# Attention's matmuls inside a product instead of between two products, in a hybrid decoder block

## The chip, the cores and the metric

The kernel runs on one core of a Trainium2 chip. The time is the device time of one execution in microseconds (us), and the number compared is the median over several runs of the same program. A run that is profiled also leaves a trace, in which every instruction of the core's engines has a start and a duration: PE (TensorE matmuls), PEld (TensorE weight loads), DVE (VectorE), ACT (ScalarE), POOL (GpSimd) and SP (SyncE, which only issues DMAs here).

## What is computed

One layer of a decoder block on a sequence of 2048 positions with 1024 channels, in float32. Cut to what matters:

```python
h = rms_norm(x, norm_g)
u = h @ w_in                       # (2048, 1024) @ (1024, 8704)
v_c, b_c, c_c, z_c, q, k, v, z_a, gate_logits = split(u)
y_c = b_c * causal_depthwise_conv(c_c * v_c, conv_w) * silu(z_c)
y_a = y_c @ w_conv_out
q, k = rms_norm(q, per head), rms_norm(k, per head)     # 16 query heads, 4 key heads of 64
o = sliding_window_attention(q, k, v, sinks) * silu(z_a)  # window 128, blocks of 128
y_b = o @ w_attn_out
g_a, g_b = split(sigmoid(gate_logits + gate_b))
out = x + (g_a * y_a + g_b * y_b) @ w_out
```

In the attention each block of 128 queries meets its own block of keys and the one before it: scores, a mask, a softmax with one sink for each head, and the product of the probabilities with the values.

## The kernel before

**Precision.** A float32 operand is split into a high and a low part (fp32r), and a product is the sum of three matmuls: high with high, high with low, low with high. Every matmul comes with its own weight load of 128x128.

**Projections.** The sequence is worked in two tiles (t = 0 and 1) of 1024 positions. A projection of 256 output channels by 1024 positions is a unit. A unit is computed with seven products instead of eight, on sums of quarters of its operands. One product (`product`, line 454) is twelve matmuls of 128x512 into one PSUM bank: four chunks of the contraction by the three terms above. Between the products ACT and DVE copy, add and evacuate the banks (X, V and the single bank Y).

**The order of the work.** `run` (line 734) steps through the units. One step, a *tick*, issues one product on TensorE and then the tasks that stand in a table for this tick: every other task of the program was put there by `put(tick, task)`, and the table `PLACES` shifts some of them by a few ticks. All engines work in program order, so a task's place in the table is its place in the queue of each engine that it uses. Waits between engines are semaphores that follow from the tiles: an instruction that writes a tile waits for the last readers of what was in that buffer.

**Attention.** There are 64 blocks of attention work (2 tiles, 4 key heads, 8 blocks of 128 positions, all four query heads of the key head at once). Each is a chain of tasks, set from a tick n:

- n-5: `att_load`, DMAs on SP bring the queries and keys (tiles `q2`, `kq`, and `lows`, which has two fixed buffers).
- n: `att_scores` (line 1090). Six matmuls, the *scores*, are issued in a row: for each half h one of 128x384 (line 1099) and two of 128x192 (line 1103), into a PSUM tile `s` of two banks. The pool `ps_s` has a single buffer of it. Then DVE masks the tile, takes the row maxima (a reduction that reads `s`) and four small operations.
- n+1: `att_exp` (line 1125 and 1128). ACT computes the exponentials out of `s`, four instructions of 128x128, each followed by the read of its sum (ACTIVATION_READ_ACCUMULATOR). After the last of them the tile `s` is free.
- n+2 to n+10: DVE normalizes and transposes in 32x32 squares, POOL sends the result through DRAM (`fd`) and back (`x`), ACT and DVE split it, and POOL cuts it to the window with four selections (line 1175), the last of which completes `xl`.
- n+13: `att_values` (line 1186). Six matmuls of 128x256 in a row, the *values*, into a bank `po` of the pool `ps_m` with three buffers.
- n+14: `att_out` (line 1197): ACT copies two quarters of `po`; n+15: DVE adds the other two and SP stores.

A row of matmuls that a task issues stands on TensorE after the product of its tick and before the product of the next one. So in the program order of TensorE the scores stand as six in a row between two products, and so do the values.

Of the kernel before, what the change touches and what calls it, by code (L numbers as in the profile page):

```python
# [8 lines left out]
F32 = mybir.dt.float32  # L9
# [6 lines left out]
P = 128  # L16
# [5 lines left out]
NB = T // P  # L22
# [3 lines left out]
HD = 64  # L26
# [63 lines left out]
        (1, (1, 1), (1, 1), (0, 0)), (3, (1, 0), (1, 0), (1, 1)))  # L90
LD_SUM, SUM_STEP, Z_SUM = 3, 1, 1
N_ROOT, N_RB, N_STEP, W_AT = 36, 2, 10, 18
OP_FROM, OP_STEP, OP_LD = 3, 2, 5

V_, F_, B_, X_, L_, O_, S_ = 4, 2, 4, 9, 10, 13, 15
# [4 lines left out]
def block_kernel(  # L100
# [350 lines left out]

    B_AT = {(0, 0): 1, (1, 0): 2, (0, 1): 8, (1, 1): 3}

    def product(ps, u, n, ops, start):
        force(u, n)
        hi, lo = ready[u][n]
        for j in range(KP):
            b = ops[n][j]
            for i, (w, m) in enumerate(((hi, 0), (hi, 1), (lo, 0))):
                nc.tensor.matmul(  # L460
                    ps, lhsT=w[:, j, :], rhs=b[:, m, :],
                    start=start and j == 0 and i == 0, stop=j == KP - 1 and i == 2,
                    skip_group_check=not start)
        d = done.setdefault(u, set())
        d.add(n)
        live[0] -= sum(c for m, c in USES if n in m and m <= d)
# [267 lines left out]
    def run(gen):  # L734
        while True:
            tick[0] += 1
            if next(gen, gen) is gen:
                tick[0] -= 1
                return
            ahead_loads()  # L740
            hi, lo = (piece() if tick[0] >= W_FROM else None) or (None, None)
            if hi:
                hi()

            fs = at.pop(tick[0], [])
# [341 lines left out]
        nc.sync.dma_start(v4[LH].rearrange("p (i x) -> p i x", i=2), pairs)  # L1087
        return v2

    def att_scores(t, j, b, ld):  # L1090
        first = t * NB + b == 0
        nm = f"{t}_{j}_{b}"
        q2, kq, kz = ld
        rv = rqs[t, j][:, b // HB, b % HB]
        sp = ps_s.tile([P, 2, 2, 2 * P], F32, tag="s", name=f"s{nm}")
        for h in range(2):
            skip = (2 - h) * HD if first else 0
            keys = slice(h * HD + skip, (h + 3) * HD)
            nc.tensor.matmul(
                sp[:, h, :, skip : 3 * HD], lhsT=kq[:, 1, h * P : (h + 1) * P], rhs=kz[:, :, keys],  # L1100
                start=True, stop=False)
            for c in range(2):
                nc.tensor.matmul(  # L1103
                    sp[:, h, c, skip : 3 * HD], lhsT=q2[:, h, c, :], rhs=kq[:, 0, keys],
                    start=False, stop=c == 1)
# [14 lines left out]
        add(st[:, 2], sink_r[:, j].rearrange("p h c -> p (h c)"), st[:, 1])  # L1120
        return sg, st, rv
# [63 lines left out]

    def att_values(t, j, b, pcv, v2):
        xh, xl, y = pcv
        po = mbank(f"po{t}_{j}_{b}").rearrange("p g q -> p (g q)")
        for h in range(2):
            cs = slice(h * 2 * P, (h + 1) * 2 * P)  # L1190
            for n, (kind, xx) in enumerate(((2 + h, xh), (h, y), (2 + h, xl))):
                nc.tensor.matmul(  # L1192
                    po[:, cs], lhsT=v2[:, kind, :], rhs=xx[:, h],
                    start=n == 0, stop=n == 2)
        return po

    def att_out(t, j, b, po):
        pov = po.rearrange("p (h e s c q) -> p h e s c q", h=2, e=2, s=2, c=2)
        o = slot([P, 2, P], F32, f"o{t}_{j}_{b}")
        parts = []  # L1200
        for e in range(2):
            own, oth = HALVES[e], HALVES[1 - e]
            ov = o[own].rearrange("p c (h s q) -> p h s c q", h=2, s=2)
            nc.scalar.copy(ov, pov[oth, :, e])  # L1204
            parts.append((ov, pov[own, :, e]))
        return o, parts
# [526 lines left out]
    def attention(t, places):  # L1733
        for r, n in enumerate(places):
            j, b = divmod(r, NB)
            got = {}
            n += PLACES.get(f"a{t}.{r}", 0)

            def step(k, f, got=got):
                def g():  # L1740
                    got[k] = f(got)
                return g

            put(n - 5, step("l", lambda g, j=j, b=b: att_load(t, j, b)), f"a{t}.{r}.l")
# [219 lines left out]
```

## Time and profile before

| | |
|---|---|
| median of 3 runs | 1906.28 us (1903.66 to 1906.4) |
| profiled execution, its own time | 1902.79 us |
| its span, first to last instruction | 1901.1 us |
| PE busy | 1886.4 us of the span, 8646 matmuls |
| DVE, ACT, POOL busy | 1588.3, 1000.3, 646.1 us |
| granted TensorE clock | 1.000 |
| score matmuls / value matmuls | 384 / 384, in 64 rows of six each |

The page of the profile gives busy time for each engine, the waits give who waited for whom and how long, and the timeline gives single instructions: start, duration, engine, line of the code, operation, tile written and tiles read, shapes, and in brackets the idle time just before it with what ended it. Two things are to be kept in mind. Matmuls are pipelined and their recorded ends are modelled, so what a matmul costs is read from start to start, not from its duration. And the idle time of an engine that others do not wait for costs nothing.

### The profile page before, as it was taken

Reading aid. Unit: us, or ns where it says so; the run is one execution under the profiler, and the core shown is the slowest. Engines: PE = TensorE matmul, PEld = TensorE weight load, DVE = VectorE, ACT = ScalarE, POOL = GpSimd, SP = SyncE. Lnnn points to the kernel's source line nnn. Section 1 sums busy time; section 2 is a strip of 40 time slices with the busy share of each in tenths; the row PEclk is TensorE's granted clock in tenths of the full one; section 3 lists DMA queues with packets and bytes.
Section 4 is the critical chain, followed back from the end, with each engine's and each line's share of the span. In section 5 each row is a group of like instructions: output and inputs, shape, how many; then the busy total and the mean of one; then the engine's idle time right before and its main releaser. Section 6 shows DMA issues by size and latency. Waiting matters only on the chain.

```text
span 1901.1 us, 27689 instructions
## 1 busy us (share of the span) xinstructions
PE 1886.4 (99%) x8646; PEld 1567.7 (82%) x8646; DVE 1588.3 (84%) x2670; ACT 1000.3 (53%) x1989; POOL 646.1 (34%) x930
## 2 busy tenths in 40 slices
PE   9999999999999999999999999999999999999999
PEld 7888888888888888888878888888887888888887
DVE  7989989898889889877799888888888868878654
ACT  7565455457767345435465554556665435535221
POOL 2073335335565001123273444445565001223000
PEclk9999999999999999999999999999999999999999
DMA  8286555568888966778387554578887844879553
GB/s 307 65 240 190 157 158 171 172 196 281 252 251 253 314 238 210 253 185 263 101 236 215 164 166 146 162 222 261 285 250 228 280 151 152 274 167 290 187 173 108
DMA packets 228644, 398.05 MB, mean 209 GB/s; under 512 B 31312, under 2 KB 106064, under 8 KB 228496
## 3 DMA queue, kind: packets, MB, share of 16 engines
q1 hardware_dynamic: 191104, 295.27, 47.9%
q0 software_dynamic: 37248, 100.97, 19.5%
q8 instruction: 69, 1.13, 0.3%
q14 instruction: 79, 0.65, 0.1%
q10 hardware_dynamic: 144, 0.03, 0.0%
HBM read 264.80 MB, written 131.35 MB: 208 GB/s over the span
## 4 chain that ended last, share of the span: by engine, by line
PE 55%; issue 6%; DMA 3%; DVE 3%; POOL 2%; ACT 1%; SPq 0%; POOLq 0%; DVEq 0%; ACTq 0%
PE Y L460 19%; PE Vcv L460 2%; PE Xcv L460 2%; PE Vo L460 2%; PE Xo L460 2%; PE Vza L460 2%; PE Xza L460 2%; PE yb L1399 2%; PE Vya L460 1%; PE Vz L460 1%; PE Xz L460 1%; PE Vb L460 1%; PE Yya L460 1%; PE Xga L460 1%; PE Vga L460 1%
## 5 line engine op out<-in xcount | busy, mean ns | idle before, releaser
L1155 POOL DMA_DIRECT2D x<-fd x256 | 139.7, 552 | 138.1 <-DMA fd<-f 58.0
L1175 POOL TENSOR_SCALAR_AFFINE_SELECT xh<-xh 64x512 fp32r<-64x512 f32 x64 | 69.6, 1088 | 151.1 <-DVE xl L253 118.3
L1128 ACT ACTIVATE p<-s,st,rq 128x128 f32<-128x128 f32 x256 | 112.8, 450 | 2.4 <-DMA fd<-f 2.4
L1148 POOL DMA_DIRECT2D fd<-f x64 | 37.2, 581 | 190.0 <-DVE f L253 175.8
L1460 POOL DMA_DIRECT2D mt<-thya x32 | 28.3, 883 | 117.3 <-DVE thya L253 106.0
L1175 POOL TENSOR_SCALAR_AFFINE_SELECT xl<-xl 64x512 fp32r<-64x512 f32 x64 | 65.5, 1024 | 4.4
L921 POOL DMA_DIRECT2D q2d<-q_h x64 | 44.2, 691 | 56.6 <-ACT q_h L913 48.1
L359 ACT CAST wcv_sh<-wcv_raw 128x1024 fp32r<-128x1024 f32 x16 | 16.8, 1052 | 85.5 <-DVE wcv_raw L253 85.5
L1175 POOL TENSOR_SCALAR_AFFINE_SELECT yp<-yp 64x512 fp32r<-64x512 f32 x64 | 59.4, 928 | 4.2
L1175 POOL TENSOR_SCALAR_AFFINE_SELECT yp<-xl 64x512 fp32r<-64x512 f32 x64 | 56.5, 883 | 3.1
L253 DVE TENSOR_TENSOR o<-po,o 64x256 f32<-64x256 f32 x128 | 53.5, 418 | 2.6 <-ACT o L1204 1.5
L253 DVE SCALAR_TENSOR_TENSOR y<-u,cols,y 128x512 f32<-128x512 f32 x64 | 50.5, 795 | 4.2 <-ACT y L1242 3.0
L253 DVE TENSOR_TENSOR p<-p,st 128x512 f32<-128x512 f32 x64 | 51.3, 801 | 2.8 <-DVE st L253 0.3
L1204 ACT COPY o<-po 64x256 f32<-64x256 f32 x128 | 46.9, 367 | 11.0 <-PE po L1192 4.2
L921 POOL DMA_DIRECT2D q2d<-q_l x64 | 44.1, 689 | 22.7 <-DVE q_l L253 8.0
L1128 ACT ACTIVATION_READ_ACCUMULATOR p<-s,st,rq 128x1 f32 x256 | 50.8, 198 | 0.0
L1374 POOL DMA_DIRECT2D c1f<-ocd x12 | 6.5, 543 | 121.3 <-DMA thb<-gd 116.4
L1103 PEld LDWEIGHTS s<-kq,q 128*128 128x128 f32 x256 | 45.9, 189 | 2.2
L253 DVE STREAM_TRANSPOSE f<-p 128x512 f32<-128x512 f32 x64 | 45.4, 710 | 2.7 <-DVE p L253 0.2
L253 DVE TENSOR_TENSOR xl<-x,xh 128x512 fp32r<-128x512 f32 x64 | 43.7, 683 | 4.6 <-DMA fd<-f 4.0
L1374 POOL DMA_DIRECT2D c0f<-ocd x12 | 6.5, 544 | 116.9 <-DVE zain L253 102.0
L1103 PE MATMUL s<-kq,q 128*128 128x192 f32 (+2 forms) x256 | 46.2, 262 | 0.0
(880 smaller groups left out, 6677.5 us busy)
## 6 DMA issues: line engine op xcount, KB each, us to landing
gd<-th SPq DMA_DIRECT2D x64, 256.0 KB, 3.1
wcv_raw<-in_w_in SPq DMA_DIRECT2D x32, 512.0 KB, 4.3
q<-q2d SPq DMA_DIRECT2D x64, 256.0 KB, 4.3
v<-vd SPq DMA_DIRECT2D x128, 128.0 KB, 3.8
fd<-f POOLq DMA_DIRECT2D x64, 256.0 KB, 4.3
x<-fd POOLq DMA_DIRECT2D x256, 64.0 KB, 3.7
x<-in_x SPq DMA_DIRECT2D x16, 512.0 KB, 6.4
wga_raw<-in_w_in SPq DMA_DIRECT2D x16, 512.0 KB, 5.0
```

The lines of the kernel that those rows point to most:

```text
L253: r = f(*args, **kw)
L359: return (lambda: nc.scalar.copy(hi, src), lambda: vec.tensor_tensor(out=lo, in0=src, in1=hi.bitcast(F32), op=ALU.subtract))
L460: nc.tensor.matmul(ps, lhsT=w[:, j, :], rhs=b[:, m, :], start=start and j == 0 and i == 0, stop=j == KP - 1 and i == 2, skip_group_check=n ...
L921: nc.gpsimd.dma_start(q2d[t][j][half, q * 2 * HB : (q + 1) * 2 * HB, i, e, :], src[HALVES[e]].bitcast(F32).rearrange("p (b x) -> p b x", x ...
L1103: nc.tensor.matmul(sp[:, h, c, skip : 3 * HD], lhsT=q2[:, h, c, :], rhs=kq[:, 0, keys], start=False, stop=c == 1)
L1128: nc.scalar.activation(out=p[:, i, :], in_=sg[:, i, HD : 3 * HD], func=AF.Exp, bias=st[:, 1, i : i + 1], scale=rv[:, i // 2, i % 2 : i % 2 ...
L1148: nc.gpsimd.dma_start(fd, f)
L1155: nc.gpsimd.dma_start(x[QUADS[k]], src[k])
L1175: nc.gpsimd.affine_select(out=d4, in_=s4, pattern=[[0, 4], [-32 * sg, 2], [0, 2], [-sg, 32]], compare_op=ALU.is_gt if prev else ALU.is_ge, ...
L1204: nc.scalar.copy(ov, pov[oth, :, e])
L1399: nc.tensor.matmul(ps, lhsT=w[:, j, :], rhs=b[:, l, :], start=n == 0 and m == 0, stop=n == KC - 1 and m == 2)
L1460: nc.gpsimd.dma_start(mt[t][k, :, hs(q)], m, accum_op=ALU.add)
```

## The change

The six score matmuls of a block and its six value matmuls are no longer issued by their tasks. They are put, as six small functions, into a list `between`. `product` looks into that list after each of its twelve matmuls and issues one of the functions when fewer than `EVERY` = 2 of its own matmuls are left for each function in the list. With six in the list one is issued after the 1st, 3rd, 5th, 7th, 9th and 11th matmul; with twelve, one after each.

For the scores, a new task `att_ways` at tick n-1 fills the list, so they are issued inside the product of tick n; what is left of `att_scores` stays at tick n. For the values, `att_values` stays at n+13 and fills the list, so they are issued inside the product of tick n+14. After every product `between_all` issues what may be left, and `att_out` does so too before it reads `po`. The number of instructions, their shapes and operands are the same, and so is the order on the other engines but for a few neighbouring pairs.

```diff
+EVERY = 2
...
+    between = []
+
+    def between_all():
+        while between:
+            between.pop(0)()
+
     def product(ps, u, n, ops, start):
         force(u, n)
+        left = 3 * KP
...
                     skip_group_check=not start)
+                left -= 1
+                if between and left < EVERY * len(between):
+                    between.pop(0)()
...
             if next(gen, gen) is gen:
                 tick[0] -= 1
                 return
+            between_all()
...
-    def att_scores(t, j, b, ld):
+    def att_ways(t, j, b, got):
+        first = t * NB + b == 0
+        q2, kq, kz = got["l"]
+
+        def one(h, c):
+            if (h, c) == (0, None):
+                got["p"] = ps_s.tile([P, 2, 2, 2 * P], F32, tag="s", name=f"s{t}_{j}_{b}")
+            sp = got["p"]
...
+        between.extend(lambda h=h, c=c: one(h, c) for h in range(2) for c in (None, 0, 1))
+
+    def att_scores(t, j, b, sp):
...
     def att_values(t, j, b, pcv, v2):
         xh, xl, y = pcv
-        po = mbank(f"po{t}_{j}_{b}").rearrange("p g q -> p (g q)")
-        for h in range(2):
-            cs = slice(h * 2 * P, (h + 1) * 2 * P)
-            for n, (kind, xx) in enumerate(((2 + h, xh), (h, y), (2 + h, xl))):
-                nc.tensor.matmul(
-                    po[:, cs], lhsT=v2[:, kind, :], rhs=xx[:, h],
-                    start=n == 0, stop=n == 2)
-        return po
+        got = []
+
+        def one(h, n, kind, xx):
+            if (h, n) == (0, 0):
+                got.append(mbank(f"po{t}_{j}_{b}").rearrange("p g q -> p (g q)"))
+            nc.tensor.matmul(
+                got[0][:, h * 2 * P : (h + 1) * 2 * P], lhsT=v2[:, kind, :], rhs=xx[:, h],
+                start=n == 0, stop=n == 2, skip_group_check=True)
...
     def att_out(t, j, b, po):
-        pov = po.rearrange("p (h e s c q) -> p h e s c q", h=2, e=2, s=2, c=2)
+        if not po or between:
+            between_all()
+        pov = po[0].rearrange("p (h e s c q) -> p h e s c q", h=2, e=2, s=2, c=2)
...
-            put(n, step("s", lambda g, j=j, b=b: att_scores(t, j, b, g["l"])), f"a{t}.{r}.s")
+            put(n - 1, lambda j=j, b=b, got=got: att_ways(t, j, b, got), f"a{t}.{r}.s")
+            put(n, step("s", lambda g, j=j, b=b: att_scores(t, j, b, g["p"])), f"a{t}.{r}.s")
```

How TensorE's instructions stand is seen at two places. The first is the score block of tile 0, key head 3, block 6 (the 31st of the 64). In the rows `Xz` is the PSUM bank of a product of the gate projection, `oph` its moving operand, `wz` its weights (`ah` high, `al` low), `s` the score tile, `lows`, `kq` and `q` the loaded keys and queries; the brackets name what a row waits for (DMAHW and DVE, PE, Activation and Pool semaphores). Before:

```order
L460 MATMUL Xz_0_6067<-oph_2_0_481,wz_0_ah 128x512 x2
L460 MATMUL Xz_0_6067<-oph_2_0_481,wz_0_al 128x512
L460 MATMUL Xz_0_6067<-oph_2_1_483,wz_0_ah 128x512 x2
L460 MATMUL Xz_0_6067<-oph_2_1_483,wz_0_al 128x512
L460 MATMUL Xz_0_6067<-oph_2_2_638,wz_0_ah 128x512 x2
L460 MATMUL Xz_0_6067<-oph_2_2_638,wz_0_al 128x512
L460 MATMUL Xz_0_6067<-oph_2_3_640,wz_0_ah 128x512 x2
L460 MATMUL Xz_0_6067<-oph_2_3_640,wz_0_al 128x512
L1099 MATMUL s_3_6_6205<-lows_144,kq_3_6_6022 128x2x192 [waits DMAHW2_49,DMAHW1_49,DMAHW4_49,DVE_49,DMAHW5_49,PE_49,Activation_49]
L1103 MATMUL s_3_6_6205<-kq_3_6_6022,q_0_3_6_6020 128x192 [waits DMAHW3_49,DMAHW0_49]
L1103 MATMUL s_3_6_6205<-kq_3_6_6022,q_0_3_6_6020 128x192
```

Now:

```order
L468 MATMUL Xz_0_6067<-oph_2_0_481,wz_0_ah 128x512
L1113 MATMUL s_3_6_6187<-lows_144,kq_3_6_6015 128x2x192 [waits DMAHW2_49,DMAHW1_49,DMAHW4_49,DVE_49,DMAHW5_49,PE_49,Activation_49]
L468 MATMUL Xz_0_6067<-oph_2_0_481,wz_0_ah 128x512
L468 MATMUL Xz_0_6067<-oph_2_0_481,wz_0_al 128x512
L1117 MATMUL s_3_6_6187<-kq_3_6_6015,q_0_3_6_6013 128x192 [waits DMAHW3_49,DMAHW0_49]
L468 MATMUL Xz_0_6067<-oph_2_1_483,wz_0_ah 128x512 x2
L1117 MATMUL s_3_6_6187<-kq_3_6_6015,q_0_3_6_6013 128x192
L468 MATMUL Xz_0_6067<-oph_2_1_483,wz_0_al 128x512
L468 MATMUL Xz_0_6067<-oph_2_2_638,wz_0_ah 128x512
L1113 MATMUL s_3_6_6187<-lows_144,kq_3_6_6015 128x2x192
L468 MATMUL Xz_0_6067<-oph_2_2_638,wz_0_ah 128x512
L468 MATMUL Xz_0_6067<-oph_2_2_638,wz_0_al 128x512
```

The first score matmul, with all its waits on it, moved up past eleven matmuls of the product. In 50 of the 64 blocks it stands like this, after the product's first matmul. In the other 14 the same product carries a value row too; the values come first, one after each matmul, and the first score stands after the seventh.

The second place is the value row of tile 1, key head 0, block 3 (`po` is its bank, `v` the values, `xh`, `yp` and `xl` the probabilities). Before:

```order
L460 MATMUL Vb_1_11093<-ophh_5_3_8841,wb_1_sl 128x512
L1192 MATMUL po_0_3_11108<-xh_0_3_10990,v_1_0_3_10836 128x256 [waits Pool_49]
L1192 MATMUL po_0_3_11108<-yp_0_3_10992,v_1_0_3_10836 128x256 [waits Pool_49]
L1192 MATMUL po_0_3_11108<-xl_0_3_10991,v_1_0_3_10836 128x256 [waits Pool_49]
L1192 MATMUL po_0_3_11108<-xh_0_3_10990,v_1_0_3_10836 128x256
L1192 MATMUL po_0_3_11108<-yp_0_3_10992,v_1_0_3_10836 128x256
L1192 MATMUL po_0_3_11108<-xl_0_3_10991,v_1_0_3_10836 128x256
L460 MATMUL Y<-ophh_6_0_8766,wb_1_sh 128x512 [waits Activation_49]
```

Now:

```order
L468 MATMUL Vb_1_11093<-ophh_5_3_8841,wb_1_sl 128x512
L468 MATMUL Y<-ophh_6_0_8766,wb_1_sh 128x512 [waits Activation_49]
L1214 MATMUL po_0_3_11119<-xh_0_3_10990,v_1_0_3_10829 128x256 [waits Pool_49]
L468 MATMUL Y<-ophh_6_0_8766,wb_1_sh 128x512
L468 MATMUL Y<-ophh_6_0_8766,wb_1_sl 128x512
L1214 MATMUL po_0_3_11119<-yp_0_3_10992,v_1_0_3_10829 128x256 [waits Pool_49]
L468 MATMUL Y<-ophh_6_1_8817,wb_1_sh 128x512 x2
L1214 MATMUL po_0_3_11119<-xl_0_3_10991,v_1_0_3_10829 128x256 [waits Pool_49]
L468 MATMUL Y<-ophh_6_1_8817,wb_1_sl 128x512
L468 MATMUL Y<-ophh_6_2_8863,wb_1_sh 128x512
```

The value row moved down instead: its first matmul stands one product matmul later than before, its third (the one that needs `xl`) five later, its last eleven later.

More of the change, by code (lines that the diff above doesn't have):

```diff
@@ L1088, in att_load_v @@
         return v2
-    def att_scores(t, j, b, ld):
+    def att_ways(t, j, b, got):
[5 more added lines that the diff above has]
+            sp = got["p"]
+            skip = (2 - h) * HD if first else 0
+            keys = slice(h * HD + skip, (h + 3) * HD)
+            if c is None:
+                nc.tensor.matmul(
+                    sp[:, h, :, skip : 3 * HD], lhsT=kq[:, 1, h * P : (h + 1) * P], rhs=kz[:, :, keys],
+                    start=True, stop=False, skip_group_check=True)
+            else:
+                nc.tensor.matmul(
+                    sp[:, h, c, skip : 3 * HD], lhsT=q2[:, h, c, :], rhs=kq[:, 0, keys],
+                    start=False, stop=c == 1, skip_group_check=True)
+        between.extend(lambda h=h, c=c: one(h, c) for h in range(2) for c in (None, 0, 1))
+    def att_scores(t, j, b, sp):
         first = t * NB + b == 0
         nm = f"{t}_{j}_{b}"
-        q2, kq, kz = ld
         rv = rqs[t, j][:, b // HB, b % HB]
-        sp = ps_s.tile([P, 2, 2, 2 * P], F32, tag="s", name=f"s{nm}")
-        for h in range(2):
[L1097 to L1105, printed above, removed]
         sg = sp.rearrange("p h c k -> p (h c) k")
@@ L1187, in att_values @@
         xh, xl, y = pcv
-        po = mbank(f"po{t}_{j}_{b}").rearrange("p g q -> p (g q)")
-        for h in range(2):
-            cs = slice(h * 2 * P, (h + 1) * 2 * P)
-            for n, (kind, xx) in enumerate(((2 + h, xh), (h, y), (2 + h, xl))):
-                nc.tensor.matmul(
-                    po[:, cs], lhsT=v2[:, kind, :], rhs=xx[:, h],
-                    start=n == 0, stop=n == 2)
-        return po
+        got = []
+        def one(h, n, kind, xx):
+            if (h, n) == (0, 0):
+                got.append(mbank(f"po{t}_{j}_{b}").rearrange("p g q -> p (g q)"))
+            nc.tensor.matmul(
+                got[0][:, h * 2 * P : (h + 1) * 2 * P], lhsT=v2[:, kind, :], rhs=xx[:, h],
+                start=n == 0, stop=n == 2, skip_group_check=True)
+        between.extend(
+            lambda h=h, n=n, kind=kind, xx=xx: one(h, n, kind, xx)
+            for h in range(2) for n, (kind, xx) in enumerate(((2 + h, xh), (h, y), (2 + h, xl))))
+        return got
     def att_out(t, j, b, po):
-        pov = po.rearrange("p (h e s c q) -> p h e s c q", h=2, e=2, s=2, c=2)
+        if not po or between:
+            between_all()
+        pov = po[0].rearrange("p (h e s c q) -> p h e s c q", h=2, e=2, s=2, c=2)
         o = slot([P, 2, P], F32, f"o{t}_{j}_{b}")
```

## The prediction

> **What bounds the kernel now.** I read the page first, for the share of each engine and the clock, then the waits of TensorE, then its timeline at the places of the change, then ACT's and the DMAs' rows beside them.
>
> ```profile
> PE 1886.4 (99%) x8646; PEld 1567.7 (82%) x8646; DVE 1588.3 (84%) x2670; ACT 1000.3 (53%) x1989; POOL 646.1 (34%) x930
> ...
> PEclk9999999999999999999999999999999999999999
> ```
>
> TensorE is busy 99% of the span at full clock: it sets the end, and whatever makes its stream longer or shorter moves the time one for one. Its waits are next to nothing (who waited for whom; us in total, times, longest):
>
> ```profile
> PE po L1192 <- POOL xl L1175: 1.0, 2, 0.8
> ...
> PE s L1099 <- DMA lows<-kd: 0.9, 1, 0.9
> ```
>
> So the change can gain on two things only: what the small matmuls cost TensorE by standing in rows, and 1.0 us of waits for `xl`. It can lose by new waits. The number and shape of the instructions stay.
>
> **The small matmuls.** Costs are read from start to start. A product after which nothing disturbs TensorE, tile 0:
>
> ```profile
> 573.28 0.62 PE L460 MATMUL Xz<-oph,wz_ah 128*128 128x512 f32 x2
> ...
> 576.00 0.33 PE L1099 MATMUL s<-lows,kq 128*128 128x384 f32 x1
> ```
>
> Twelve matmuls take 576.00 - 573.28 = 2.72 us, 0.227 each. A score row and the product behind it:
>
> ```profile
> 1116.85 0.33 PE L1099 MATMUL s<-lows,kq 128*128 128x384 f32 x1
> ...
> 1117.62 0.66 PE L460 MATMUL Vb<-ophh,wb_th 128*128 128x512 f32 x2
> 1118.12 0.39 PE L460 MATMUL Vb<-ophh,wb_tl 128*128 128x512 f32 x1
> ...
> 1120.42 0.84 PE L460 MATMUL Y<-ophh,wb_d 128*128 128x512 f32 x3
> ```
>
> The six scores take 0.77 us (1116.85 to 1117.62), and the product behind them 2.80 instead of 2.72: its first two matmuls take 0.50 instead of 0.45. So a score row costs 0.77 + 0.08 = 0.85 us. A value row:
>
> ```profile
> 1107.95 0.28 PE L1192 MATMUL po<-xh,v 128*128 128x256 f32 x1
> ...
> 1108.66 0.63 PE L460 MATMUL Y<-ophh,wb_sh 128*128 128x512 f32 x2
> 1109.13 0.39 PE L460 MATMUL Y<-ophh,wb_sl 128*128 128x512 f32 x1
> ...
> 1111.41 0.39 PE L460 MATMUL Xb<-ophh,wb_ah 128*128 128x512 f32 x1
> ```
>
> 0.71 for the six and 2.75 for the product behind them: 0.74 in all. Both rows stream 1536 columns; at the product's own rate, 2.72 us for 6144 columns, 1536 columns take 0.68. This bounds the gain: at most (0.85 - 0.68) + (0.74 - 0.68) = 0.23 us a block, 64 x 0.23 = 14.7 us. The other bound: a score row makes the two matmuls behind it 0.05 longer, a value row 0.02 (0.47 for two). If each single small matmul did that to its own neighbours, six scores would cost 0.77 + 6 x 0.05 = 1.07, six values 0.71 + 6 x 0.02 = 0.83: 0.31 us more a block, 64 x 0.31 = 20 us lost. I take a small gain, half of the two tails, (0.08 + 0.03) / 2 x 64 = 3.5, rounded to **-3 us**: nearest is the value row, whose matmuls already run at 0.12 us each, close to what their 256 columns take at the product's rate (0.113), with a tail of 0.03. Standing alone cannot make them much cheaper.
>
> The Trainium skill ("TensorE: Matmul & The Clock Gate", the section "Step-by-step: what each phase is for") says that TensorE pulls a weight load ahead of the matmuls in flight. By that rule, a small matmul's load hides behind the long matmul ahead of it, and a block would cost only its columns: the whole 14.7 us. The rows say that most of it is hidden already; no run so far has a small matmul between two long ones, so this stays a rival.
>
> **The waits that go.** In the value rows `xl` is now needed after five matmuls of the product, some 1.1 us of product later than its place in a row. The quoted wait of 1.0 us, longest 0.8, goes: **-1 us**.
>
> **The waits that come.** The first score matmul carries all waits: for the loads of `lows` and `kq`, and for ACT, which must have read the last of the block before out of `s`, since there is one buffer. It now stands after the product's first matmul: eleven matmuls, 11 x 0.227 = 2.5 us, earlier. TensorE works in order, so if it waits there, eleven matmuls of the product wait behind it, then the ACT or DVE evacuation of that product. The program around it moves in step (the 0.85 us of the row are spent inside the product instead of behind it), so I hold ACT's rows where they are and ask whether they end before the new place. In the block above (the 31st) the product starts at 573.28, so the new place is 573.28 + 0.23 = 573.51. ACT's exponentials of the block before:
>
> ```profile
> 573.28 0.46 ACT L1128 ACTIVATE p<-s,st,rq 128x128 f32<-128x128 f32 x1 [2.44 <-DMA fd<-f]
> ...
> 574.94 0.21 ACT L1128 ACTIVATION_READ_ACCUMULATOR p<-s,st,rq 128x1 f32 x1
> ```
>
> The last one ends at 574.94 + 0.21 = 575.15. With 0.13 us from a releaser to the matmul (the 13th block below: the load lands at 352.8 + 4.3 = 357.1, the matmul starts at 357.24), TensorE waits 575.15 + 0.13 - 573.51 = 1.77 us where it waited nothing. The same reading for four more blocks, the last read of `s` by ACT and the first score:
>
> ```profile
> 498.03 0.21 ACT L1128 ACTIVATION_READ_ACCUMULATOR p<-s,st,rq 128x1 f32 x1
> 498.98 0.33 PE L1099 MATMUL s<-lows,kq 128*128 128x384 f32 x1
> 525.93 0.20 ACT L1128 ACTIVATION_READ_ACCUMULATOR p<-s,st,rq 128x1 f32 x1
> 527.37 0.33 PE L1099 MATMUL s<-lows,kq 128*128 128x384 f32 x1
> 1276.63 0.21 ACT L1128 ACTIVATION_READ_ACCUMULATOR p<-s,st,rq 128x1 f32 x1
> 1277.80 0.33 PE L1099 MATMUL s<-lows,kq 128*128 128x384 f32 x1
> 1297.95 0.21 ACT L1128 ACTIVATION_READ_ACCUMULATOR p<-s,st,rq 128x1 f32 x1
> 1300.00 0.34 PE L1099 MATMUL s<-lows,kq 128*128 128x384 f32 x1
> ```
>
> The new places are 2.5 us ahead of the scores (3.2 in the last, where a value row of 0.72 lies between): 496.49, 524.88, 1275.31, 1296.79. The waits: 1.88, 1.39, 1.66, 1.49. Five smaller ones of this kind, read likewise, are 0.43, 0.37, 0.51, 0.67 and 1.02. Sum of the ten with 1.77: 11.2 us. In the other blocks ACT is done in time. The loads, two blocks (columns: issue times and the time to landing):
>
> ```profile
> L1068 SPq DMA_DIRECT2D lows<-kd x2: 468/532/596, 352.3 to 352.8; - x2
> ...
> DMA to landing us min/median/max: 2.8/3.6/4.3
> 357.24 0.41 PE L1099 MATMUL s<-lows,kq 128*128 128x384 f32 x1 [0.95 <-DMA lows<-kd]
> L1068 SPq DMA_DIRECT2D lows<-kd x2: 468/472/477, 531.5 to 532.2; - x2
> ...
> DMA to landing us min/median/max: 4.0/4.2/4.3
> 537.13 0.33 PE L1099 MATMUL s<-lows,kq 128*128 128x384 f32 x1
> ```
>
> The first is one of the 14 where values go ahead: new place 354.98, landing 357.1, wait 2.25 where it was 0.95. The second: place 534.61, landing 536.2, wait 1.74. Two more, 1.16 and 0.63. Sum 5.8, less the 0.95 of before, 4.8. Together 11.2 + 4.8 = 16.0 us in 14 blocks. Some will be shared: a wait of TensorE gives ACT, DVE and SP time, and where a second block follows within four products (527.37 and 537.13; the block 10 us before 1277.80) the first wait shortens the second, by up to 1.39 and 0.63. That leaves **+14 us**. Below, this term is bounded by half of it, 7, if every wait brings ACT as far ahead as it cost; above by some 25, if later evacuations push ACT: a product with scores in it ends 0.85 later, and so its first copy.
>
> The values end later now, near the end of their product. ACT's copy of `po` is in the next tick's tasks, behind that product's own evacuation, and ACT is busy 53%. I cost it at nothing; where ACT comes early it is late by up to 2.5 us, and with it the exponentials behind it, which is part of the 25.
>
> **The sum.** -3 - 1 + 14 = +10 us. The profiled execution took 1902.8 (span 1901.1 and 1.7 around it), so 1912.8 on its terms. The three runs lay 0.9 to 3.6 above it, 2.7 on average: I predict **1915 us**. For this kernel about 0.2%, 3.8 us, can be told from no change.
>
> **The rivals.**
>
> *The waits dissolve, no change* (chance 0.2). ACT and DVE settle ahead after the first waits, half the waits remain: -3 - 1 + 7 = +3, 1908. For it: DVE is 84% busy, ACT 53%, so neither must lag; the blocks with waits come in pairs. Against it: ACT's 2.44 us before the exponentials at 573.28 are owed to a DMA that POOL issues, not to TensorE, so a wait of TensorE there moves nothing ahead.
>
> *The loads hide, faster* (0.15). A block falls from 1.59 us (0.85 + 0.74) to its columns, 1.36: -14.7 - 1 + 7 = -9, 1896. It decides against the full 14 us of waits only from a block cost under 1.59 - 13 / 64 = 1.39 us, nearly the floor; with half the waits under 1.49. For it: the score row is 0.17 above its columns. Against it: the value row is only 0.06 above, and the small matmuls that follow each other at 0.12 already have their loads beside matmuls.
>
> *Each single matmul disturbs its neighbours, much slower* (0.15). +20 from the second bound, or the waits at 25: 1902.8 + 2.7 + 20 - 1 + 14 = 1939, or with the waits alone -3 - 1 + 25, 1927. For it: the first two matmuls behind a row are the slow ones, and now every product matmul has a small neighbour. Against it: a row of six is followed by a tail no longer than 0.08, so this may be paid for the row, not for each.
>
> *The change does not do what it says*: the orders show each small matmul behind a product matmul, so this has no chance worth a number.
>
> **How the numbers follow.** Forecast 0.5, own range 1909 to 1922. The range 1898 to 1927 takes in the first rival, half of the second and the lower half of the third; about 0.15 is left out. Faster by over 0.2% is the second rival, 0.15; within 0.2%, the first, 0.2; slower, 0.65.
>
> **What would show it.** TensorE's waits should have a new group at the scores, for ACT's `p`, of some 10 us in about ten places around 420 to 580 and 1265 to 1390, and one for `lows` of 3 to 6 us; the group for `xl` should be gone. A product with six small matmuls should take 2.72 + 0.71 to 0.85 from start to start where it doesn't wait. The forecast is wrong if the waits for ACT stay under 4 us, or if a product with six scores takes 3.4 us (the loads hide) or 3.8 (the neighbours suffer) instead of 3.5 to 3.6.

## The result and the profile after

The changed kernel took **1935.9 us** (median of six runs, 1931.94 to 1937.0); the kernel before, on the same chip, 1905.25 (six runs, 1901.53 to 1908.9). The ratio is 1.0155 with a 95% interval of 1.0145 to 1.0166: 30.7 us slower, where 10 us were forecast. The sign was right, the time lies outside the range. The profiled execution took 1934.37 us, its span is 1932.7, 31.6 longer than before.

The page of the changed kernel, its first rows:

```profile
PE 1900.8 (98%) x8646; PEld 1569.9 (81%) x8646; DVE 1588.8 (82%) x2670; ACT 1000.8 (52%) x1989; POOL 647.8 (34%) x930
...
PEclk9999999999999999999999999999999999999999
```

Instructions and busy time of DVE, ACT and POOL are what they were. TensorE is busy 14.4 us longer (1900.8 - 1886.4), and the other 17 us of the longer span are gaps. The digits of the clock hide what is shown further down. Who TensorE waited for (us in total, times, longest):

```profile
PE s L1113 <- ACT p L1149: 7.6, 6, 2.3
PE s L1113 <- DMA lows<-kd: 3.9, 2, 3.0
PE Vz L468 <- DVE wz_sl L254: 2.9, 4, 1.3
PE Y L468 <- DVE q_t L254: 2.0, 1, 2.0
...
PE Y L468 <- DVE st L254: 1.5, 1, 1.5
PE Vz L468 <- ACT wz_sh L360: 1.3, 2, 1.0
PE Y L468 <- DVE zs L254: 1.0, 1, 1.0
```

The first two groups were forecast, and the group for `xl` is gone as forecast. Those of the groups below them that are longer than before were not forecast (`q_t` stood in the list before with 1.7): they are waits at a product's own matmuls, with no small one waiting. I call them waits of the products themselves.

To split the 31.6 us I took the time from each matmul's start to the next one's. Where two shapes follow each other undisturbed this has a fixed value (0.227 us for 128x512); what is over it by more than 0.15 us I count as a wait. The waits so counted are 39.0 us, against 13.6 before, so 25.4 more; 6.5 come from products without a wait, and 25.4 + 6.5 = 31.9. What matmuls lost while the clock was halved stands in a row of its own. By cause:

| | forecast | measured |
|---|---|---|
| small matmuls standing singly | -3 | +6.5 |
| waits for `xl` | -1 | -1.4 |
| waits at a block's first score | +14 | +14.8 (15.9 in 14 blocks, before 1.1) |
| the products themselves wait | 0 | +7.7 |
| TensorE at half its clock | not seen | +4.3 |
| sum | +10 | +31.9 |

The same account along the program. The start of the same product matmul in both traces is subtracted (us by which a kernel lags behind the one before; the kernels of the last four columns are those of the experiments below):

```
before, us     change   values   values   scores   scores
                        only     early    only     from 7th
 222             1.1      0.8      0.7      1.5      1.0
 342             4.0      1.7      1.5      3.7      1.3
 467             8.6      3.3      1.5     11.8      5.0
 593            16.3      7.2      4.3     21.4      6.7
 651            20.2     10.1      6.1     21.2      6.3
 976            20.2     10.1      6.2     21.3      6.3
1035            21.5     14.5      6.1     21.5      8.8
1216            23.3     15.3      8.3     21.6      9.1
1340            29.1     16.2     10.3     31.4     11.0
1525            31.9     17.2     11.9     33.4     12.2
1896            32.0     17.2     11.9     33.4     12.2
```

Nearly all of it is lost where attention runs; in 325 us without it (651 to 976) and after 1525 nothing is. The exception lies between 976 and 1035, ahead of the second tile's first scores (1024.4 before): there every kernel, the one before included, has one wait of a product for DVE's `q_t`. From start to start it is 1.89 us before, 2.15 in the change and 3.90 with the values alone. DVE in turn waited for a DMA (`k_b<-krd`: 1.01, 1.26 and 3.02 us). With the half clock behind it this place makes 4.4 of the 17.2 us of the values alone. One execution varies by a few us: that of the values alone was the slowest of its four, 1919.95 against a median of 1917.01.

**Half the clock.** Three stretches of the changed kernel (us of the stretch, its length, busy PE, PEld, DVE, ACT and POOL with their instructions, the granted clock, DMA):

```profile
505.01:508.42 3.41, 1.07 (x5) 0.66 (x4) 2.02 (x5) 3.36 (x13) 1.86 (x3) 1.00 0.66 212
508.42:511.83 3.41, 3.41 (x11) 2.76 (x10) 2.98 (x4) 2.11 (x4) 1.58 (x2) 0.50 0.81 268
511.83:515.24 3.41, 3.41 (x17) 2.84 (x16) 2.25 (x7) 0.57 (x1) 0.59 (x1) 1.00 0.93 268
```

In the first stretch TensorE waited at a first score (timeline: start, duration, idle time before it and releaser):

```profile
507.72 0.44 PE L1113 MATMUL s<-lows,kq 128*128 128x384 f32 x1 [2.34 <-ACT p L1149]
```

In the next it is granted half its clock and gets 11 matmuls done; in the third 17. There are three such stretches of 3.41 us in the changed kernel, from 361.65, 508.42 and 1017.01, and none before but at the very end. By the spacing of the matmuls in them they cost about 1.45, 1.45 and 1.35 us. The first two stand behind waits at scores, the third behind the wait for `q_t`, which the kernel before has too, a little shorter.

### The profile page after: what moved, and what is told of

Read it like the earlier page. It is cut to its first block, busy times and chain, and to the rows that moved or that the text cites. A ratio compares the mean times of both kernels' runs of the same rounds, so it can differ in the third digit from the quotient of the medians.

```text
span 1932.7 us, 27628 instructions
## 1 busy us (share of the span) xinstructions
PE 1900.8 (98%) x8646; PEld 1569.9 (81%) x8646; DVE 1588.8 (82%) x2670; ACT 1000.8 (52%) x1989; POOL 647.8 (34%) x930
## 4 chain that ended last, share of the span: by engine, by line
PE 72%; DVE 10%; issue 7%; DMA 5%; ACT 4%; POOL 2%; SPq 1%; DVEq 0%; POOLq 0%; ACTq 0%
PE Y L468 27%; PE Vcv L468 4%; PE Xcv L468 4%; PE Vo L468 2%; PE Xo L468 2%; PE yb L1427 2%; PE Vza L468 2%; PE Xza L468 2%; PE Xb L468 2%; PE po L1214 2%; PE Xz L468 2%; PE Vz L468 2%; PE Vq L468 1%; PE Vb L468 1%; PE Vgb L468 1%
## 5 line engine op out<-in xcount | busy, mean ns | idle before, releaser
L1196 POOL TENSOR_SCALAR_AFFINE_SELECT xh<-xh 64x512 fp32r<-64x512 f32 x64 | 66.2, 1035 | 172.8 <-DVE xl L254 111.3
L1117 PE MATMUL s<-kq,q 128*128 128x192 f32 (+2 forms) x256 | 64.4, 252 | 0.0
L1232 ACT COPY o<-po 64x256 f32<-64x256 f32 x128 | 47.0, 367 | 25.7 <-PE po L1214 21.7
L1113 PE MATMUL s<-lows,kq 128*128 128x384 f32 (+2 forms) x128 | 44.2, 345 | 13.6 <-ACT p L1149 7.6
L254 DVE TENSOR_REDUCE st<-s 128x4 f32<-128x512 f32 x64 | 44.2, 690 | 2.0
```

What stands on the lines that cost most here:

```text
L254: r = f(*args, **kw)
L1113: nc.tensor.matmul(sp[:, h, :, skip : 3 * HD], lhsT=kq[:, 1, h * P : (h + 1) * P], rhs=kz[:, :, keys], start=True, stop=False, skip_group_ ...
L1117: nc.tensor.matmul(sp[:, h, c, skip : 3 * HD], lhsT=q2[:, h, c, :], rhs=kq[:, 0, keys], start=False, stop=c == 1, skip_group_check=True)
L1196: nc.gpsimd.affine_select(out=d4, in_=s4, pattern=[[0, 4], [-32 * sg, 2], [0, 2], [-sg, 32]], compare_op=ALU.is_gt if prev else ALU.is_ge, ...
```

## The experiments

Each kernel is the changed one with the edit shown, which is shortened. Times are medians; in each group of four the kernel before ran on the same chip (1905.78, 1905.26 and 1905.07).

**Values alone, scores alone.** In the first the scores are a row between two products again, as before; in the second the values are.

```diff
-put(n - 1, lambda: att_ways(t, j, b, got))
-put(n, step("s", lambda g: att_scores(t, j, b, g["p"])))
+put(n, step("s", lambda g: att_row(t, j, b, g)))   # att_ways, between_all, att_scores
```

```diff
 def att_values(t, j, b, pcv, v2):
+    kept = between[:]
+    between.clear()
     between.extend(...)
+    between_all()
+    between.extend(kept)
```

> The values inside the product as in the changed kernel, the scores as a row at tick n as before. Theory A (TensorE waits at the first score for ACT or for the loads, and what follows from these waits): no such waits here, the wait for xl gone (-1.5 us), the single matmuls at the price that undisturbed products of the changed kernel show, 0.07 us a block: +4.7; sum +3 us. Theory B (the values end later, so ACT waits for po, and the evacuations and weight casts behind it come late): +8 to +12 us, with ACT waiting some 20 us at its copies of po. Theory C (small matmuls between long ones cost much more than in a row): half of the loss, +15 us.

> The scores inside the product as in the changed kernel, the values as a row after the product of tick n+13 as before. Theory A: the waits at the scores stay, 15 us, with one or two stretches of half clock after the longest (1.7 us each) and 1.7 us for the single matmuls: +18 to +22 us. Theory B: ACT's waits for po fall back to about 4 us and 8 us of the loss go, so also some +20, but the waits at the scores get smaller too, since the exponentials stand behind the copies: under 12 us. Theory C: half of the loss, +15 us, most of it in products without a wait.

Values alone: 1917.01, ratio 1.0059 (1.004 to 1.0079), 11 us slower. Scores alone: 1933.78, 1.0146 (1.0127 to 1.0165), 28 us, almost the whole loss. So both parts lose, and not additively: 11 + 28 is more than 31. TensorE's first waits with the scores alone:

```profile
PE s L1113 <- ACT p L1149: 12.9, 15, 2.3
PE s L1113 <- DMA lows<-kd: 6.6, 2, 4.6
```

From start to start, with what the half clock added at the scores themselves, they waited 26.9 us here and 17.4 in the whole change (some 23.6 and 15.9 without it), but there the products themselves waited more. One block shows the exchange. The 31st waited 2.30 us with the scores alone, and the clock was halved behind it. In the whole change it waited 0.30, but 6 us ahead of it a product had waited 1.42 for `wz_sl`, and in that time ACT could come ahead.

**Rows, but the values late.** Nothing stands inside a product; the scores are at their old place, the values one product later than before.

```diff
-EVERY = 2
+EVERY = 0
```

> EVERY = 0: nothing is issued inside a product; both sets stand as rows again, the scores behind the product of tick n as before, the values behind the product of tick n+14, one product later than before. Theory A: no waits at the scores, same time as before within 3 us. Theory B: ACT waits for po as in the changed kernel or somewhat more, +8 us. Theory C: same time as before.

1921.85, ratio 1.0084 (1.0068 to 1.01): 16 us slower with not one matmul inside a product. Lateness of the values is a cause by itself. Who waited for the matmuls that write `po` (all instructions of that tile; us in total, times):

```profile
  ACT o L1232: 23.7, 12
  ACT zs L1334: 14.5, 3
  POOL x L1176: 9.1, 2
  ACT p L1149: 3.8, 1
  ACT L1334: 3.5, 1
...
  DVE f L254: 2.7, 1
```

The same view of the kernel before:

```profile
  POOL x L1155: 22.8, 5
  ACT zs L1306: 7.7, 2
  ACT o L1204: 7.0, 3
```

ACT's copy `o` reads `po`. The others do not: DVE's `f` is the transposition of `p`. What it can wait for at `po` is only the buffer it writes: the probabilities `xh`, `yp`, `xl` and the values `v` stand in the same pool of 19 buffers, from which `f`, `x`, `p` and `zs` are taken in turn. A value matmul that comes a product later frees its operands a product later.

The sum of these waits does not measure the loss: without `o` it is 34 us before, 40 here and 26 in the changed kernel. What counts is whether a wait is handed on to TensorE. In the changed kernel I followed the waits of the products themselves back through the engines' busy stretches to the idle time behind them. The four from 615 to 631 (1.65, 1.18, 0.45 and 0.70 us from start to start, 4.0 together) go back to ACT or DVE waiting for `po` at a buffer: `p`, `f`, `zs` and `zs`. The others go back to a DMA or to a product. So the way through the buffers is shown for 4.0 us there; how the 16 us of this kernel divide between buffers and copy was not separated.

**All small ones from the 7th matmul on.**

```diff
-EVERY = 2
+EVERY = 1
```

> EVERY = 1: in a product with six the first small matmul stands after the seventh of the twelve instead of after the first, 1.36 us later; products with twelve are as in the changed kernel. Theory A: each wait at the scores in the 50 blocks shrinks by up to 1.36 us, the sum from 16 to about 5 us, and no half clock follows there: +30 becomes +12 to +17 us. Theory B: the values end as late as in the changed kernel, so 8 us stay for that. Theory C: the same number of single matmuls, +30 us as in the changed kernel.

This moves only the six of a product that carries six; the products with twelve stay as in the change. 1929.71, ratio 1.0123 (1.0102 to 1.0143): 6 us less than the change. The waits for ACT's `p` fell to 1.7 us, but the products themselves waited more: `Y` 12.8 and `Vz` 11.6 from start to start, against 9.9 and 5.3.

**Three mends, singly and together.** The copies of `po` one tick later; the tile `s` as two tiles of one bank; the loads one tick earlier; all three.

```diff
-put(n + O_ + 1, step("z", ...att_out...))
-put(n + S_, step("t", ...att_sum...))
+put(n + O_ + 2, step("z", ...att_out...))
+put(n + S_ + 1, step("t", ...att_sum...))
```

```diff
-got["p"] = ps_s.tile([P, 2, 2, 2 * P], F32, tag="s")
+got.setdefault("p", []).append(ps_s.tile([P, 1, 2, 2 * P], F32, tag=f"s{h}"))   # one for each h
```

```diff
-put(n - 5, step("l", ...att_load...))
+put(n - 6, step("l", ...att_load...))
```

> Changed kernel, with ACT's copies of `po` (and the sums behind them) set one tick later, at n+15 and n+16, so that the values, which now end inside the product of n+14, have ended before ACT reaches the copy. Theory A (late values hold up ACT, which then comes late with weight splits and evacuations that plain products wait for): ACT's waits for `po` fall from 21.7 us to under 6, the waits in products without small matmuls go (some 7 us), and the time falls by 6 to 10 us against the changed kernel, to 1926 to 1930. Theory B (ACT comes late because of its exponentials, which have moved with the scores; the wait for `po` is idle time that ACT could spare): no change, 1934 to 1938.

> Changed kernel, with the score tile `s` as two tiles of one PSUM bank each, one for each half h, so that the first score matmul waits for the first two exponentials of the block before alone, and the fourth for the last two; DVE masks and reduces each half by itself (two instructions more each). Theory A (the single buffer of `s` is what the first score waits for): the waits of scores for ACT's `p`, 7.6 us in the list of waits and some 10 from start to start, fall under 4; the time falls by 6 to 11 us, to 1925 to 1930. Theory B (the block as a whole is late, and what the scores gain is waited for elsewhere, or DVE's extra instructions make ACT late): under 3 us gained, 1933 to 1938.

> Changed kernel, with the loads of queries and keys issued one tick earlier, at n-6 instead of n-5. Theory A (the loads land later than the new place of the first score): the waits for `lows` (3.9 us in the list) go, and with the longest, 3.2 us, the 3.41 us at half clock that follow it, worth 1.6: the time falls by 4 to 7 us, to 1929 to 1932. Theory B (the earlier loads are issued behind the same DMAs, or the block waits for ACT next): under 2 us gained, 1934 to 1937.

> Changed kernel with all three: the copies of `po` a tick later, `s` in two tiles, the loads a tick earlier. Theory A (three separate causes of waits, and beside them some 6.5 us that single small matmuls cost from start to start): the waits fall to the 13 us of the kernel before, what is left is the 6.5 us, so 1909 to 1916, and no window at half clock but the last. Theory B (the waits stand in for each other, or come from the rate at which ACT and DVE work): 1920 or more.

None gained. Later copies: 1940.02, ratio 1.0183 (1.0167 to 1.0199). Two tiles: 1937.16, 1.0158 (1.0138 to 1.0178). Earlier loads: 1943.92, 1.0203 (1.0188 to 1.0219). All three: 1944.25, 1.0206 (1.0187 to 1.0224). The first theory of each falls as far as the time goes. The traces say why.

With the later copies ACT's `o` no longer waits for `po` (21.7 us in the changed kernel), and still the products themselves waited as long as there (`Y` 11.3 us from start to start against 9.9, `Vz` 5.1 against 5.3). So their waits don't hang on that copy. Who waited for `po` there:

```profile
  ACT p L1149: 2.7, 1
  POOL x L1176: 2.5, 1
  ACT L1334: 2.4, 1
...
  DVE f L254: 1.5, 1
```

The list adds up to 13 us, against 48 in the changed kernel and 41 before, and the kernel is the slower one: waiting less for `po` did not make it faster. Some waits for reused buffers stayed, and others stand behind other readers, as here, where DVE's `zs` waits at its buffer for the DMA that reads `f`, and TensorE, at 601.06, for `zs` (1.84 us):

```profile
600.31 0.69 DVE L254 TENSOR_TENSOR zs<-Y,s5z 128x512 f32<-128x512 f32 x1 [4.59 <-DMA fd<-f]
```

What made this kernel slower than the change was not followed further. A wait for `po` at a buffer in the changed kernel, with what follows on DVE, ACT and TensorE (three views, in this order):

```profile
615.71 0.69 DVE L254 TENSOR_TENSOR p<-p,st 128x512 f32<-128x512 f32 x1
617.89 0.71 DVE L254 STREAM_TRANSPOSE f<-p 128x512 f32<-128x512 f32 x1 [1.50 <-PE po L1214]
...
622.26 0.68 DVE L254 TENSOR_TENSOR zs<-Y,s5z 128x512 f32<-128x512 f32 x1
```

```profile
618.48 1.28 ACT L1334 ACT_TABLE_LOAD   x1 [2.84 <-PE po L1214]
```

```profile
617.52 0.28 PE L1214 MATMUL po<-xh,v 128*128 128x256 f32 x1
```

The transposition starts when the fourth value matmul, the last to read `xh`, has ended (617.52 + 0.28 = 617.80). DVE stood still for 1.50 us, ACT for 2.84, and DVE's addition of `Y` into `zs` comes late; TensorE, whose next product needs the one bank `Y`, waited 1.18 us at 622.99. Before, the same transposition stood right behind its input:

```profile
598.40 0.69 DVE L253 TENSOR_TENSOR p<-p,st 128x512 f32<-128x512 f32 x1
599.23 0.71 DVE L253 STREAM_TRANSPOSE f<-p 128x512 f32<-128x512 f32 x1
```

With two tiles the waits for ACT's `p` fell from 7.6 to 4.8, but the products of `Y` waited 15.3 us from start to start instead of 9.9, and `Vz` 7.5 instead of 5.3. With the earlier loads the wait of 3.2 us at 361.83 went, and at 502.56 that kernel was 5.2 us ahead of the changed one (507.72 there). It lost it again, and more, at one place:

```profile
PE s L1113 <- DMA lows<-kd: 9.8, 1, 9.8
```

```profile
1441.64 4.54 SPq L1240 DMA_DIRECT2D od<-o  x2
...
1450.18 1.10 SPq L1080 DMA_DIRECT2D lows<-kd  x2
```

In SP's queue the loads of that block were issued behind two stores, while TensorE stood at the block's first score from 1444.3 to 1454.2. Why the stores came late there was not followed further.

**Apart from the late values.** What the mends were worth may have been covered by the late values. So the next four take causes apart: the values early, and not late, with the scores as rows; the scores alone with two tiles; the scores alone from the 7th matmul on; and a whole mended version (values early, two tiles, the loads of tile 0 earlier). The earlier loads were not tried by themselves again.

```diff
-put(n + O_, step("o", ...att_values...))       # values early, on "values only"
+put(n + O_ - 1, step("o", ...att_values...))
```

```diff
-EVERY = 2                                      # scores from the 7th, on "scores only"
+EVERY = 1
```

```diff
-put(n - 5, step("l", ...att_load...))          # mended: with the values early and the two tiles
+put(n - 5 - (t == 0), step("l", ...att_load...))
```

> The kernel with the values alone inside a product (scores as rows, as before), but issued one tick earlier, inside the product of n+13, so that they end 0.7 us before their old place and not 2 us behind it. Theory A (late values are what costs: ACT waits for `po`, and whoever reuses the buffers of `xh`, `yp`, `xl` and `v` in the ring of 19 waits for the same matmuls): waits of ACT, DVE and POOL for `po` fall from some 48 us to the 24 of the kernel before, the waits in plain products go; what is left is 64 x 0.073 = 4.7 us of single small matmuls, and some waits for `xl`, which is needed up to 2 us earlier: 1909 to 1914, against 1917 for the values alone. Theory B (what costs is that a product with values in it ends 0.74 us later, and its evacuation with it): 1916 to 1920, and plain products wait as they did.

> The kernel with the scores alone inside a product (values as rows at their old place), with `s` in two tiles of one bank, one for each half. Theory A (the single buffer makes the first score wait, and no late values mask it here): waits of scores for ACT's `p` fall from 12.9 to 3 to 6 us, and the time from 1934 to 1922 to 1927. Theory B (as with the split in the whole change: what is gained there is waited for elsewhere): 1930 to 1936.

> The kernel with the scores alone inside a product, but from its 7th matmul on, one after each, instead of after the 1st, 3rd and so on: the first score stands 6 matmuls, 1.36 us, later. Theory A (what costs is how far the first score was moved up): the 26.9 us of score waits, each 1.36 shorter or gone, fall to some 7, the windows at half clock with them; the single small matmuls cost 1.7 us more: 1914 to 1920, against 1934. Theory B (the loss comes from the scores being single, or from ACT and DVE at large): 1928 or more.

> The whole change, mended: values one tick earlier, `s` in two tiles, the loads of tile 0 one tick earlier. Theory A (late values, the place of the first score and the loads are the causes): 6.5 us for single small matmuls, some 5 us of score waits and 2 to 4 us for `xl`: 1916 to 1922, against 1936. Theory B (waits stand in for each other, whatever is mended): 1930 or more. Either way not under the kernel before.

*Values early*: 1915.28, ratio 1.0053 (1.0038 to 1.0068), 10 us slower. The time lies between the two theories; the traces decide. Who waited for `po` most (us in total, times), and what TensorE waited for:

```profile
  POOL x L1184: 8.0, 3
  ACT o L1240: 3.8, 2
  ACT zs L1342: 3.5, 1
```

```profile
PE po L1222 <- POOL yp L1204: 3.3, 7, 1.1
```

The waits of others for `po` add up to 18 us, less than before (41 by this view; the expectation's 24 comes from the list of waits, its 48 from this view), and the waits of the products themselves are back to the size they had (`Y` 5.9 from start to start, 5.5 before). That speaks for the lateness. The time alone does not: the ratio, 1.0053, cannot be told from the 1.0059 of the values alone. What replaced them is TensorE waiting for POOL's selections at the values, 8.5 us from start to start against 1.4. The span is 11.9 us longer: 4.7 for single matmuls and 7.1 for those waits. So the place of the values has no slack on either side: later holds buffers, earlier waits for POOL.

*Scores alone with two tiles*: 1921.87, ratio 1.0088 (1.0072 to 1.0103), 12 us less than with one tile; the waits for ACT's `p` fell from 12.9 to 5.5:

```profile
PE s L1113 <- ACT p L1151: 5.5, 6, 1.7
```

*Scores alone from the 7th matmul on*: 1912.75, ratio 1.0041 (1.0027 to 1.0056), 21 us less than from the first. This is the best kernel with anything inside a product, still 7.7 us slower than before:

```profile
PE s L1113 <- DMA lows<-kd: 2.7, 1, 2.7
PE s L1113 <- ACT p L1149: 2.3, 5, 0.8
```

The scores waited 7.5 us from start to start, as theory A worked out (some 7), where they had waited 26.9. How far the first score is moved up decides.

*Mended*: 1927.82, ratio 1.0119 (1.0103 to 1.0134): 8 us less than the change, 6 to 12 more than theory A gave. The values waited 10.2 us from start to start for POOL, the scores 8.2. No version came under the kernel before.

## Why the prediction was right or wrong

**What bounds the kernel, right.** TensorE's stream sets the end: the 31.9 us counted at its matmuls are the lag of the end (32.0 in the table of the lags).

**"I take a small gain, half of the two tails: -3", wrong.** A product with scores and one with values in the changed kernel, where nothing waits:

```profile
190.27 0.39 PE L468 MATMUL Vcv<-oph,wcv_th 128*128 128x512 f32 x1
...
191.13 0.25 PE L1117 MATMUL s<-kq,q 128*128 128x192 f32 x1
191.22 0.65 PE L468 MATMUL Vcv<-oph,wcv_th 128*128 128x512 f32 x2
191.71 0.26 PE L1117 MATMUL s<-kq,q 128*128 128x192 f32 x1
...
193.85 2.88 PE L468 MATMUL Y<-oph,wcv_d 128*128 128x512 f32 x12
196.57 0.62 PE L468 MATMUL Xb<-oph,wb_ah 128*128 128x512 f32 x2
```

```profile
1475.23 0.39 PE L468 MATMUL Vz<-ophh,wz_th 128*128 128x512 f32 x1
...
1478.73 2.92 PE L468 MATMUL Y<-ophh,wz_d 128*128 128x512 f32 x12
1481.49 0.61 PE L468 MATMUL Xz<-ophh,wz_ah 128*128 128x512 f32 x2
```

They take 3.58 and 3.50 us, in the interval named (2.72 + 0.71 to 0.85) or just over it. But the product behind still has a tail: 2.74 in the median behind scores (2.72 here), 2.76 behind values. In all a score block costs 0.880 (as a row 0.853) and a value block 0.813 (0.740): 64 x (0.027 + 0.073) = 6.4 us lost, where the account above leaves 6.5, about a third of the way to the upper bound of 20. The row of a small matmul shows how: from 191.13 to 191.71 one 128x192 and two 128x512 take 0.58, where their columns at the product's rate take (192 + 1024) x 2.72 / 6144 = 0.54. A long matmul beside a small one is no longer at its 0.227: behind a 128x192 it takes 0.255 in the median of the changed kernel.

The prediction weighed the Trainium skill here ("TensorE: Matmul & The Clock Gate", the section "Step-by-step: what each phase is for"): a weight load is pulled ahead of the matmuls in flight. By that rule alone the small matmuls would have cost only their columns. These rows do not bear that out for a small matmul between long ones.

**"-1" for `xl`, right**: 1.4 from start to start.

**"+14" for the first scores, right in sum.** It measured 14.8. By blocks it was rough: for the five blocks worked out at ACT's rows, 1.77, 1.88, 1.39, 1.66 and 1.49 were forecast, and 0.30, 2.51, 0.56, 1.30 and 2.20 came; for the two loads 2.25 and 1.74, and 3.19 and 1.00 came. The sharing that the prediction took off is there (0.30, 0.56), and at 1417.28 came 1.66, where outside the five nothing over 1.02 was forecast for ACT. So it is in part luck that the sum came out. The scores alone, at the same place, waited 26.9 us (some 23.6 without the half clock), near the upper end of 25: which of the two came depended on how much others made TensorE wait.

**"I cost it at nothing", the step that failed.** The values ending later were costed at ACT's copy of `po` alone, as a part of the 25. The late values by themselves cost 16 us as rows and 11 inside products, of which 4.7 are single matmuls (and in the traced execution 4.4 of 17.2 the wait for `q_t`). The copy alone is not what decides (the later copies changed nothing for the better): the operands of the values are buffers of a ring that the other engines write in turn, and a late reader holds up whoever is next in the ring. In the whole change the products themselves waited 7.7 us more, where nothing was forecast; 4.0 us of waits there go back to `po` by way of a buffer, and for the rest the way stays open.

**Not seen: the clock.** 4.3 us here, 8.9 with the scores alone. A wait of 2.1 us or more was priced at its length; where it fell into one step of the clock, another 1.35 us or more stood behind it. Of the 4.3 us, 2.9 stand behind scores.

The rivals: the waits did not dissolve and the loads did not hide. The third, 1939, came nearest in time, but by its mechanism (each single matmul at +20 over) it has only the 6.5 us; what the forecast lacks beyond them are two causes that no rival named, the waits of the products themselves and the clock.

## What to carry to other kernels

A row of small matmuls between two products looks like a break in the stream, but what it costs over its columns can be read from start to start, and here it was smaller than what single small matmuls cost. Before an instruction is moved, list not only what it waits for but whom it lets go: a reader that comes later keeps its operands' buffers, and in a pool that is handed round, the next writer is on another engine and has nothing to do with it in the code. A wait on the bounding engine that is mended may only hand its place to the next one; to size one cause, take the others away first.

## What the runs showed of the hardware

The half clock comes in steps of 3.41 us on a fixed grid: the three stretches start 43.0 and 149.0 such steps apart ((508.42 - 361.65) / 3.413 and (1017.01 - 508.42) / 3.413). I summed for each step of the fourteen traces the time that TensorE waited in it. Leaving out the first 10 us, and of the others taking the steps at full clock: all 25 with 2.1 us or more of waits were followed by a step at half clock, of ten between 1.9 and 2.1 us five were, and of 31 between 1.5 and 1.9 none. It is the sum within a step that counts, so a wait that lies across two steps can go free: at 1325.55 the changed kernel waited 2.20 us, with 1.46 in one step, and kept its clock:

```profile
1324.21:1327.62 3.41, 2.07 (x11) 1.82 (x12) 2.41 (x6) 2.94 (x9) 1.45 (x3) 1.00 0.97 298
1327.62:1331.03 3.41, 3.41 (x19) 2.88 (x19) 2.30 (x6) 1.63 (x2) 3.16 (x5) 1.00 1.09 285
```

With the scores alone the same block waited 2.18 us, 2.29 in one step with the small gaps around it, and the next step was at 0.50. The Trainium skill ("TensorE: Matmul & The Clock Gate", the section "What's actually happening") gives a free-running window of 3413 ns, which these traces agree with. It says that the clock halves after an idle window of that length; here some 2 us of waits in a window that was otherwise busy were enough.
